# Attention keys written once and copied into both partition halves by DMA, W_u folded during the gates, first biases issued behind V's copies

## The chip, the cores and the metric

The kernel runs on one core of a Trainium2 chip. The metric is the device time of one execution in microseconds (us). The core's engines each run their own list of instructions, in the order of that list: PE (TensorE, matmuls; PEld is its weight loads), DVE (VectorE), ACT (ScalarE), POOL (GpSimd) and SP (SyncE, which here issues DMAs). PSUM tiles (`ps_mm`, `ps_o`, `ps_s`, `ps_t`) hold matmul results.

## The reference

One layer of an encoder over two request groups that share the weights, a prompt of 1024 tokens and a sample of 512, each with 16 meta tokens in front; width 1024, all in float32. Cut to what matters:

```python
h = rmsnorm(x, g_mix)
z = h @ w_in                        # 1024 -> 3*512 + 512 + 2*1024
q, k, v, u, gate_na, gate_fn = split(z)
# 8 heads of 64. A grid token (64 columns a row) attends to the nearest
# 8 rows x 16 columns and the 16 meta tokens; scores have a bias by offset.
y_na = neighbourhood_attention(q, k, v, rel_bias, meta_bias) @ w_branch_na
# u in 4 groups of 128 channels: real part of the 2-D DFT over positions and channels
y_fn = fourier_mix(u) @ w_branch_fn
mixed = sigmoid(gate_na) * y_na + sigmoid(gate_fn) * y_fn
x = x + mixed @ w_out
a = relu(rmsnorm(x, g_mlp) @ w_up)
y = rmsnorm(x + (a * a) @ w_down, g_final)[16:]     # meta tokens dropped
```

## The kernel before

Every float32 factor is kept as two tiles, a rounded high part and the rest (`hi` and `lo`, or `kh` and `kl`), and a product is three matmuls: hi x hi, hi x lo, lo x hi (`mm3`, L120; within attention L491 to L493). Splitting a result out of PSUM takes one instruction on ACT for hi (L131) and one on DVE for lo (L132).

The sample's layer runs first, then the prompt's. Its stages: norm and transpose; V's projection; attention; the gates; `merge_na`, which multiplies attention's output by its branch weights; the Fourier branch (`fourier_channels`, `fourier_positions`); `merge_fn`; the output projection and the MLP.

**Attention** goes over four pairs of heads, `pr` 0 to 3. The generator `project(pr)` makes queries and keys of a pair: the key product in chunks (two of 264 columns for the sample, three of 352, 344 and 344 for the prompt), then the query product, 512 columns at a time. Each head's keys are needed in both halves of the 128 partitions, since a query tile packs two rows of blocks there. A pair has eight units per row block (two heads by four column blocks `j`). A unit is: two matmuls for the scores (L588, L589); on DVE the bias is added (L593), ACT takes the exponential (L595), DVE the reciprocal and the scaling (L596, L597); PE transposes the result (L601), ACT and DVE copy it from PSUM (L131, L132), and PE multiplies by V (L618). These steps of different units are interleaved by `step` with fixed lags, and between them `feed` advances a second chain of work, the next pair's `project` or, in the last pair, extra work: `fold_u` and some column blocks of the gates done early (`early_gates`, as many as `quota` says).

V is written to DRAM (`vd_sample`), spread there into block order (`spread_v`, L692, `vf_sample`), and read back per unit (L555, `vr`). The bias tile `bm` of a unit is a DMA from a prepared table (L706).

**The folds** multiply weights by other weights. `fold_u` multiplies W_u by the channels' DFT matrix: 2 MB of W_u in tile `wuT`, eight groups of four matmuls (L244), each split by three instructions on ACT and three on DVE, two stores of 256 KB a group to the DRAM tiles `wu`. It works in a pool of its own (`fold`) that is open during sample attention. `folded` reads `wu` back through DMAs that POOL issues (L787). `fold_fn` (L756) adds and subtracts two weight tables on DVE: eight blocks `dm`, each with two loads of 256 KB (`in_w_fnA`, `in_w_fnB`), two DVE instructions (L765) and a store to `wfn` (L767). It is one of the generators of the list `beside`, each of which the gates advance once per block `dm`.

**What sets the order.** A tile scheduler takes the program and puts each engine's instructions into a fixed order when the kernel is built; pools' lifetimes and buffer counts bear on it. SP issues nearly all DMAs, one after the other; POOL issues some. `self.behind(marks)` keeps what is written in its block behind the marked instructions.

The key part of `project` writes every chunk, per head, into both halves by engine instructions, for each half `hp`:

```python
nc.scalar.copy(out=flat[hh][hp, gs], in_=src[:, m:])
nc.vector.tensor_tensor(out=flat[2 + hh][hp, gs], in0=src[:, m:],
                        in1=flat[hh][own, gs].bitcast(F32), op=ALU.subtract)
```

and for the first chunk two more for the meta tokens' copies (L527, L532).

Of the kernel before, what the change touches and what calls it, by code (L numbers as in the profile page):

```python
# [17 lines left out]
F32 = mybir.dt.float32  # L18
# [4 lines left out]
ALU = mybir.AluOpType  # L23
# [45 lines left out]
class Layer:  # L69
# [163 lines left out]
    def fold_u(self, p):  # L233
# [3 lines left out]
        dm = p.tile([128, 128], F32, name="dftc")  # L237
        nc.sync.dma_start(dm, self.ins["dft_ch"])
        wuT = p.tile([128, 4, D], F32, name="wuT")
        nc.sync.dma_start(wuT, self.ins["w_uT"].rearrange("(g p) d -> p g d", p=128))  # L240
        for kt in range(8):
            ps = self.psum("mm")
            for g in range(4):
                nc.tensor.matmul(ps[:, g * 128:(g + 1) * 128], wuT[:, g, kt * 128:(kt + 1) * 128], dm,  # L244
                                 start=True, stop=True)
            psv = ps.rearrange("p (g c) -> p g c", g=4)
            hi = p.tile([128, 512], F32R, name="wu_hi", bufs=2)
            lo = p.tile([128, 512], F32R, name="wu_lo", bufs=2)
# [79 lines left out]
    def run(self, order):  # L328
# [3 lines left out]
        for i, (name, T) in enumerate(order):  # L332
# [20 lines left out]
            else:  # L353
                w0 = self.qk_weights(0, [[att.tile(s, F32R, name=n, tag=n, bufs=4).rearrange(
                    "p a b -> p (a b)" if n == "kh" else "p a -> p a")[:, :D].rearrange("p (a b) -> p a b", a=8)
                    for _ in range(2)] for n, s in (("kh", [128, T // 64 + 2, 64]), ("q", [128, T]))])
# [117 lines left out]
    def attention(self, p, name, T, hT, w0, after):  # L474
# [22 lines left out]
        def project(pr):  # L497
# [3 lines left out]
            kh = [p.tile([128, nslot, 64], F32R, name="kh", tag="kh", bufs=4) for _ in range(2)]  # L501
            kl = [p.tile([128, nslot, 64], F32R, name="kl", bufs=4) for _ in range(2)]
            state[pr] = (qs, kh, kl)
            for t in kh + kl:
                for s in (0, nslot - 1):
                    nc.gpsimd.tensor_copy(t[:, s, 16:64].rearrange("p (g c) -> p g c", g=2)[:, :, 0:8],
                                          self.zero[:, None, 0:8].to_broadcast([128, 2, 8]))

            def copies(t, q):

                return bass.AP(t.tensor, t[q].offset, [list(t[q].ap[0]), [(nslot - 1) * 64, 2], [24, 3], [1, 16]])

            for ci, (c0, cn) in enumerate(kch):
                ps = self.psum("mm" if pr else None)
                yield from product(ps[:, :cn], wk, slice(c0, c0 + cn))
                m = NM if ci == 0 else 0
                t0 = 64 + c0 + m - NM
                gs = slice(t0, t0 + cn - m)
                flat = [t.rearrange("p s c -> p (s c)") for t in kh + kl]
                for hh in range(2):  # L520
                    own = slice(64 * hh, 64 * hh + 64)
                    both = own, slice(64 - 64 * hh, 128 - 64 * hh)
                    src = ps[own, :cn]
                    for hp in both:
                        nc.scalar.copy(out=flat[hh][hp, gs], in_=src[:, m:])
                        if m:
                            nc.scalar.copy(out=copies(kh[hh], hp), in_=src[:, None, None, :m].to_broadcast([64, 2, 3, 16]))  # L527
                    for hp in both:
                        nc.vector.tensor_tensor(out=flat[2 + hh][hp, gs], in0=src[:, m:], in1=flat[hh][own, gs].bitcast(F32),
                                                op=ALU.subtract)  # L530
                        if m:
                            nc.vector.tensor_tensor(out=copies(kl[hh], hp), in0=src[:, None, None, :m].to_broadcast([64, 2, 3, 16]),  # L532
                                                    in1=copies(kh[hh], own).bitcast(F32), op=ALU.subtract)
                yield
# [35 lines left out]
        def unit(pr, hh, R, j, blk, shared):  # L570
# [10 lines left out]
            qs, kh, kl = state[pr]  # L581
            bm = p.tile([128, wide], F32, name="bm", bufs=8 if T == 512 else 4)
            self.bias(bm, h, j, w, b)
# [4 lines left out]
            nc.tensor.matmul(ps[:, :W], qs[hh][:, qc], kh[hh][:, kw[0], kw[1]], start=True, stop=False)  # L588
            nc.tensor.matmul(ps[:, :W], qs[hh][:, qc], kl[hh][:, kw[0], kw[1]], start=False, stop=True)  # L589
# [51 lines left out]
        self.spread_v(name, blocks)  # L641
        for _ in project(0):
            pass
# [3 lines left out]
        quota = (0, 0, 0, 1) if T == 512 else (4, 2, 2, 4)  # L647
# [13 lines left out]
        for pr in range(4):  # L661
            nxt = chain(project(pr + 1) if pr < 3 else after, islice(early, 8 * quota[pr]))
            steps = 8 * (quota[pr] + (T // 512 + len(kch) if pr < 3 else 1)) + 4
# [820 lines left out]
```

## Time and profile before

| | |
|---|---|
| runs | 2087.53, 2093.07, 2096.18 us; median 2093.07 |
| profiled execution | 2095.71 us; span 2093.9 us, mean granted clock 0.985 |
| PE busy | 2012.8 us, 96% of the span |
| DVE, ACT, POOL busy | 1115.2, 717.0, 801.3 us |
| sample attention, pairs 0 to 3 | begin 70.0, 95.0, 119.0, 143.2 us; end 180.3 us |
| sample gates, then merge_na | 180.3 to 270.6 us, to 293.0 us |
| prompt attention | about 820 to 1040 us |
| DMA queues, share of 16 engines | hardware (SP) 246.24 MB, 37.8%; software (POOL) 15.37 MB, 3.0% |

How to read it: a row of the timeline has the start, the duration, the engine, the line, the operation, its tile written from its source tiles, the shape, the number of instructions and, in brackets, how long the engine was idle ahead of it and for what. Matmuls overlap in a pipeline, so the price of one is the distance between starts, not its duration. A table by stage gives busy time of each engine in each stretch, the granted TensorE clock (1.00 is full), and the share of time that the DMA engines were busy. A row of DMA queues or issues gives the time from issue to landing. Idle time of an engine matters only where PE waits for it.

### The profile page before, as it was taken

What the parts mean: (1) busy time and instruction counts of PE and PEld (TensorE: products, weight loads), DVE (VectorE), ACT (ScalarE), POOL (GpSimd) and SP (SyncE); (2) the same over time, 40 slices, a digit from 0 to 9 for tenths busy, and PEclk for the clock granted to TensorE, in tenths of its full rate; (3) what the DMA queues carried; (4) which work ended last, traced back from release to release, by engine and by line L of the source; (5) the groups of instructions that cost most, each with busy time, mean ns of one, the idle gap of its engine ahead of it and who ended that gap; (6) DMA issues with size and microseconds to landing.
All of it is one profiled execution on the core that took longest, in us unless ns stands there. A gap on an engine that the chain in (4) does not pass through costs nothing.

```text
span 2093.9 us, 26781 instructions
## 1 busy us (share of the span) xinstructions
PE 2012.8 (96%) x9803; PEld 1670.9 (80%) x9803; DVE 1115.2 (53%) x2073; ACT 717.0 (34%) x1311; POOL 801.3 (38%) x690
## 2 busy tenths in 40 slices
PE   6888999999999999999999999999999999999997
PEld 4777787878888878888878897877888888888886
DVE  6576035556565454577661328374333336556567
ACT  3563323333332223566542213143333332112112
POOL 3233635243443421333433226026777662222220
PEclk9989999999999999999999999999999999999999
DMA  6647753233433344434453452332333225323322
GB/s 205 195 125 219 210 157 112 71 118 106 127 92 91 101 151 173 114 108 116 130 185 116 130 153 91 131 101 86 107 109 121 94 97 203 109 91 101 101 87 95
DMA packets 244755, 263.32 MB, mean 126 GB/s; under 512 B 40904, under 2 KB 195272, under 8 KB 244456
## 3 DMA queue, kind: packets, MB, share of 16 engines
q1 hardware_dynamic: 231856, 246.24, 37.8%
q0 software_dynamic: 12768, 15.37, 3.0%
q8 instruction: 77, 1.26, 0.3%
q14 instruction: 54, 0.44, 0.1%
HBM read 212.08 MB, written 57.56 MB: 129 GB/s over the span
## 4 chain that ended last, share of the span: by engine, by line
PE 83%; DMA 5%; DVE 5%; issue 2%; ACT 2%; POOL 2%; SPq 0%; DVEq 0%; POOLq 0%; ACTq 0%
PE ps_mm L127 24%; PE ps_o L127 23%; PE ps_s L127 20%; PE ps_t L127 4%; PE ps_mm L491 3%; PE ps_mm L492 2%; PE ps_mm L493 2%; PE ps_o L618 2%; DMA raw<-in_w_fnB 1%; PE ps_t L601 1%; POOL w_lo L151 1%; DMA wfn<-raw 1%; DMA w_raw<-in_w_out 1%; PE ps_t L192 1%; PE ps_s L588 0%
## 5 line engine op out<-in xcount | busy, mean ns | idle before, releaser
L151 POOL TENSOR_TENSOR w_lo<-w_raw,w_hi 128x1024 fp32r<-128x1024 f32 x141 | 349.8, 2485 | 661.2 <-ACT w_hi L150 625.2
L150 ACT CAST w_hi<-w_raw 128x1024 fp32r<-128x1024 f32 x142 | 147.3, 1048 | 276.8 <-DMA w_raw<-in_w_up 78.6
L1026 DVE TENSOR_TENSOR relu<-relu 128x512 f32<-128x512 f32 (+1 forms) x34 | 78.9, 2322 | 120.6 <-ACT relu L1025 120.6
L491 PE MATMUL ps_mm<-hT,w_hi 128*128 128x512 f32 (+3 forms) x304 | 118.4, 390 | 0.6 <-DVE wu_lo L132 0.6
L150 ACT CAST h_hi<-w_raw 128x1024 fp32r<-128x1024 f32 x30 | 31.5, 1049 | 230.9 <-DMA w_raw<-hidden_prompt 77.2
L493 PE MATMUL ps_mm<-hT,w_lo 128*128 128x512 f32 (+3 forms) x304 | 109.9, 361 | 0.0
L492 PE MATMUL ps_mm<-hT,w_hi 128*128 128x512 f32 (+3 forms) x304 | 109.8, 361 | 0.0
L1391 DVE TENSOR_TENSOR acc<-acc,ps_mm 128x512 f32<-128x512 f32 x86 | 59.0, 686 | 38.7 <-PE ps_mm L127 38.7
L595 ACT ACTIVATE sc<-sc,ast 128x288 f32<-128x288 f32 (+4 forms) x96 | 53.9, 561 | 74.8 <-DVE ast L593 74.6
L1391 DVE TENSOR_TENSOR acc<-acc,ps_s 128x512 f32<-128x512 f32 x85 | 58.3, 686 | 39.5 <-PE ps_s L127 39.5
L1391 DVE TENSOR_TENSOR acc<-acc,ps_o 128x512 f32<-128x512 f32 x85 | 58.3, 686 | 39.4 <-PE ps_o L127 39.3
L1232 POOL TENSOR_TENSOR x<-w_hi,x 128x512 fp32r<-128x512 f32 (+1 forms) x42 | 63.8, 1518 | 39.6 <-ACT x L1235 39.6
L618 PE MATMUL ps_o<-pt,vb 104*64 104x128 f32 (+6 forms) x576 | 70.2, 255 | 6.5 <-DVE pt L132 4.8
L618 PEld LDWEIGHTS ps_o<-pt,vb 104*64 104x64 f32 (+6 forms) x576 | 65.1, 170 | 13.7 <-DVE pt L132 7.1
L559 POOL TENSOR_TENSOR vb<-vr,vb 96x384 fp32r<-96x384 f32 (+4 forms) x48 | 47.9, 1011 | 54.1 <-ACT vb L558 53.6
L593 DVE CUSTOM_DVE_ANT_0 sc<-ps_s,bm 128x288 f32<-128x288 f32 (+4 forms) x96 | 46.4, 483 | 36.4 <-PE ps_s L589 23.4
L127 PE MATMUL ps_t<-gate,x 128*128 128x512 f32 x264 | 65.3, 396 | 0.0
L493 PEld LDWEIGHTS ps_mm<-hT,w_lo 128*128 128x128 f32 x304 | 58.4, 192 | 7.8
L127 PE MATMUL ps_mm<-gate,x 128*128 128x512 f32 x256 | 64.2, 395 | 0.0
L127 PE MATMUL ps_s<-w_hi,h_hi 128*128 128x512 f32 x160 | 62.2, 389 | 0.0
L127 PE MATMUL ps_s<-w_lo,h_hi 128*128 128x512 f32 x160 | 62.2, 389 | 0.0
L127 PE MATMUL ps_o<-w_hi,h_hi 128*128 128x512 f32 x160 | 62.2, 389 | 0.0
(636 smaller groups left out, 5530.9 us busy)
## 6 DMA issues: line engine op xcount, KB each, us to landing
w_raw<-in_w_down SPq DMA_DIRECT2D x64, 512.0 KB
w_raw<-in_w_in SPq DMA_DIRECT2D x56, 512.0 KB
w_raw<-in_w_up SPq DMA_DIRECT2D x34, 512.0 KB
w_raw<-hidden_prompt SPq DMA_DIRECT2D x32, 512.0 KB
w_raw<-in_w_out SPq DMA_DIRECT2D x16, 512.0 KB
hidden_prompt<-r_hi SPq DMA_DIRECT2D x16, 512.0 KB
hidden_prompt<-r_lo SPq DMA_DIRECT2D x16, 512.0 KB
w_lo<-in_w_up SPq DMA_DIRECT2D x15, 512.0 KB
```

Source lines behind the costliest of these rows:

```text
L127: self.nc.tensor.matmul(out, a, b, start=(i == 0 and not more), stop=(i == len(terms) - 1), skip_group_check=more)
L150: nc.scalar.copy(out=hi, in_=raw)
L151: (lo_engine or nc.gpsimd).tensor_tensor(out=lo, in0=raw, in1=hi.bitcast(F32), op=ALU.subtract)
L491: nc.tensor.matmul(ps, a[0], b[0], start=(kt == 0), stop=False)
L492: nc.tensor.matmul(ps, a[0], b[1], start=False, stop=False)
L493: nc.tensor.matmul(ps, a[1], b[0], start=False, stop=(kt == 7))
L559: nc.gpsimd.tensor_tensor(out=lo, in0=vs, in1=hi.bitcast(F32), op=ALU.subtract)
L595: nc.scalar.activation(out=sc[:, :W], in_=sc[:, :W], func=AF.Exp, bias=st[:, 0:1], scale=-1.0, accum_out=st[:, 1:2])
L618: nc.tensor.matmul(po[:m, j * 128:(j + 1) * 128], v, x, start=(i == 0), stop=(i == len(ops) - 1))
L1026: nc.vector.tensor_tensor(out=r, in0=r, in1=r, op=ALU.mult)
L1232: self.nc.gpsimd.tensor_tensor(out=to, in0=x, in1=y, op=op)
L1391: nc.vector.tensor_tensor(out=acc[t][:, cs], in0=acc[t][:, cs], in1=ps, op=ALU.add)
```

## The change

- **Keys.** One tile `keys` (128 partitions: two heads by 64; hi and lo; slots; 64 columns; one buffer, in a pool of its own) is written by one ACT and one DVE instruction of 128 partitions per chunk. After the last chunk of a pair POOL issues four DMAs from it to the tiles `k` of the two heads, each into one half of the partitions (64 partitions by 1280 values for the sample, 328 KB; by 2304 for the prompt, 590 KB). The scores read `k`.
- **W_u.** `fold_u` is no longer in attention's chain; it is a generator of `beside`, in tiles that are free there, one group of four matmuls per block of the gates. The pool `fold` is gone. The reload of `wu[1, 1]` stands after the gates instead of before them.
- **Early gates.** `quota` of the sample is 2 in the last pair instead of 1.
- **Biases.** The bias of a unit of the pair's first head is issued behind the end of `spread_v` on SP.

```diff
-    def fold_u(self, p):
+    def fold_u(self, dm, wuT, places):
...
-        dm = p.tile([128, 128], F32, name="dftc")
         nc.sync.dma_start(dm, self.ins["dft_ch"])
-        wuT = p.tile([128, 4, D], F32, name="wuT")
-        nc.sync.dma_start(wuT, self.ins["w_uT"].rearrange("(g p) d -> p g d", p=128))
+        for g in range(4):
+            nc.sync.dma_start(wuT[g], self.ins["w_uT"][g * 128:(g + 1) * 128, :])
...
-            with ExitStack() as fold:
-                after = self.fold_u(fold.enter_context(pool("fold", "right"))) if i == 0 else iter(())
-                od = self.attention(att, name, T, hT, w0, after)
+            with pool(f"keys_{name}", "right") as p:
+                od = self.attention(att, p, name, T, hT, w0)
...
-                wu[1, 1] = self.folded(1, 1, wide())
+                if i == 0:
+                    beside.append(self.fold_u(
+                        mp.tile([128, 512], F32, name="relu", bufs=2)[:, :128],
+                        [t.bitcast(F32) for _ in range(2) for t in flat(self.pair(mp, [128, 2, 512]))],
+                        lambda: flat(self.pair(fn, [128, 4, 128], bufs=4))))
                 beside.append(self.fold_fn(fn))
             near_end = self.gates(T, hT, mixed, sig, lambda pr: self.weights(od[pr], oT[pr]), beside)
...
+                wu[1, 1] = self.folded(1, 1, wide())
...
-                for hh in range(2):
-                    own = slice(64 * hh, 64 * hh + 64)
-                    both = own, slice(64 - 64 * hh, 128 - 64 * hh)
-                    src = ps[own, :cn]
-                    for hp in both:
-                        nc.scalar.copy(out=flat[hh][hp, gs], in_=src[:, m:])
...
+                nc.scalar.copy(out=flat[0][:, gs], in_=ps[:, m:cn])
+                if m:
+                    nc.scalar.copy(out=copies(hi), in_=ps[:, None, None, :m].to_broadcast([128, 2, 3, 16]))
+                nc.vector.tensor_tensor(out=flat[1][:, gs], in0=ps[:, m:cn], in1=flat[0][:, gs].bitcast(F32), op=ALU.subtract)
...
+                if ci == len(kch) - 1:
+                    for hh in range(2):
+                        for half in range(2):
+                            nc.gpsimd.dma_start(ks[hh][64 * half:64 * half + 64], keys[64 * hh:64 * hh + 64])
...
-            self.bias(bm, h, j, w, b)
+            with self.behind(spread if h == 0 else []):
+                self.bias(bm, h, j, w, b)
...
         self.spread_v(name, blocks)
+        spread = self.mark((mybir.EngineType.SP,))
...
-        quota = (0, 0, 0, 1) if T == 512 else (4, 2, 2, 4)
+        quota = (0, 0, 0, 2) if T == 512 else (4, 2, 2, 4)
...
-            nxt = chain(project(pr + 1) if pr < 3 else after, islice(early, 8 * quota[pr]))
+            nxt = chain(project(pr + 1) if pr < 3 else (), islice(early, 8 * quota[pr]))
```

Three places of the built order show what moves. In these rows stand the line, the operation, the tile written and the tiles read, and the shape; lines of the changed kernel have other numbers (scores L586 and L587, the bias's addition L591, fold groups L243, `fold_fn`'s sums L768).

DVE in sample attention, where the next pair's first and second key chunks are split among the units of a pair; before, in pair 0:

```order
L593 ISA ast 128x1
L529 TENSOR_TENSOR kl<-ps_mm,kh 64x248
L532 TENSOR_TENSOR kl<-ps_mm,kh 64x2x3x16
L529 TENSOR_TENSOR kl<-ps_mm,kh 64x248
L532 TENSOR_TENSOR kl<-ps_mm,kh 64x2x3x16
L596 RECIPROCAL ast<-ast 128x1 x2
```

and in the changed kernel, from pair 1:

```order
L522 TENSOR_TENSOR keys<-ps_mm,keys 128x264
L591 ISA sc,ast<-ps_s,bm 128x216
L591 ISA ast 128x1
L594 RECIPROCAL ast<-ast 128x1
L595 TENSOR_SCALAR sc<-sc,ast 128x216
L132 TENSOR_TENSOR pt_1075<-ps_t,pt_1074 96x384
L768 TENSOR_TENSOR raw<-raw 128x256 x2
L591 ISA sc,ast<-ps_s,bm 128x288
```

The key instructions are fewer and twice as wide, and `fold_fn`'s sums, which stood in the gates, have moved up between the units of pairs 0 to 2, its loads and stores on SP with them, though no line of the diff says so.

SP between V's last store and the first read of its copies; before:

```order
L321 DMA vd_sample<-pt_420 128x512
L706 DMA bm<-g_un_273 128x1x256 x2
L706 DMA bm<-g_un_272 128x1x192 x2
L706 DMA bm<-g_un_273 128x1x256 x2
L706 DMA bm<-g_un_272 128x1x192
L321 DMA vd_sample<-pt_448 128x512
L238 DMA dftc<-in_dft_ch 128x128
L240 DMA wuT<-in_w_uT 128x4x1024
L692 DMA vf_sample_24_459<-vd_sample 9x12288 x2
L692 DMA vf_sample_32_462<-vd_sample 9x16384 x2
L144 DMA w_raw<-in_w_in 128x8x128
L555 DMA vr<-vf_sample_24_459 108x4x64
```

and in the changed kernel:

```order
L319 DMA vd_sample<-pt_420 128x512
L298 DMA vd_prompt<-vd_sample 16x2048 x2
L766 DMA raw<-in_w_fnA 128x4x128
L319 DMA vd_sample<-pt_448 128x512
L766 DMA raw<-in_w_fnB 128x4x128
L695 DMA vf_sample_24_459<-vd_sample 9x12288 x2
L695 DMA vf_sample_32_462<-vd_sample 9x16384 x2
L709 DMA bm<-g_un_272 128x1x192
L552 DMA vr<-vf_sample_24_459 108x4x64
L709 DMA bm<-g_un_273 128x1x256
L552 DMA vr<-vf_sample_32_462 96x6x64
L709 DMA bm<-g_un_273 128x1x256
```

The biases and W_u's load have left the place ahead of the spread; W_u's load now stands behind attention's last store. The loads of `fold_fn`'s first block and a small copy for the prompt's V have come in.

PE at the start of pair 3; before:

```order
L588 MATMUL ps_s<-kh,q 128x216
L589 MATMUL ps_s<-kl,q 128x216
L244 MATMUL ps_mm<-dftc,wuT 128x128 x4
L601 MATMUL ps_t<-ident,sc 96x128 x3
L244 MATMUL ps_mm<-dftc,wuT 128x128 x4
L618 MATMUL ps_o<-pt_1568,vb 128x128
```

and, in the changed kernel, the first fold group inside the second block of the gates:

```order
L127 MATMUL ps_s<-hT_81,w_lo 128x512 x2
L243 MATMUL ps_mm<-relu,w_hi 128x128
L127 MATMUL ps_mm<-hT_81,w_hi 128x512
L127 MATMUL ps_mm<-hT_82,w_hi 128x512
L127 MATMUL ps_mm<-hT_81,w_hi 128x512
L127 MATMUL ps_mm<-hT_82,w_hi 128x512
```

The fold's matmuls have left attention, where units of attention stood between them, and stand among the gates' 512-column matmuls.

More of the change, by code (lines that the diff above doesn't have):

```diff
@@ L390, in run @@
                 wide = lambda: self.pair(fn, [128, 4, 260], "wu", 1)
[L391 removed]
+                flat = lambda pair: [t.rearrange("p a b -> p (a b)") for t in pair]
+                if i == 0:
[3 more added lines that the diff above has]
+                        lambda: flat(self.pair(fn, [128, 4, 128], bufs=4))))
                 beside.append(self.fold_fn(fn))
@@ L472, in new_hT, with attention @@
         return [tuple(pool.tile([128, 8, T + extra], F32R, name=f"hT{i}") for i in range(2))]
-    def attention(self, p, name, T, hT, w0, after):
+    def attention(self, p, kp, name, T, hT, w0):
         hT, = hT
@@ L500, in project, with copies @@
             qs = [p.tile([128, T], F32R, name="q", tag="q", bufs=4) for _ in range(2)]
[L501 to L511, printed above, removed]
+            ks = [p.tile([128, 2, nslot, 64], F32R, name="k", tag="k", bufs=4) for _ in range(2)]
+            state[pr] = (qs, ks)
+            hi, lo = (keys[:, i] for i in range(2))
+            flat = [t.rearrange("p s c -> p (s c)") for t in (hi, lo)]
+            def copies(t):
+                return bass.AP(t.tensor, t.offset, [list(t.ap[0]), [(nslot - 1) * 64, 2], [24, 3], [1, 16]])
             for ci, (c0, cn) in enumerate(kch):
@@ L641, in attention @@
         self.spread_v(name, blocks)
+        spread = self.mark((mybir.EngineType.SP,))
+        keys = kp.tile([128, 2, nslot, 64], F32R, name="keys")
+        for s in (0, nslot - 1):
+            nc.gpsimd.tensor_copy(keys[:, :, s, 16:64].rearrange("p i (g c) -> p i g c", g=2)[:, :, :, 0:8],
+                                  self.zero[:, None, None, 0:8].to_broadcast([128, 2, 2, 8]))
         for _ in project(0):
```

29 lines of the change are left out of this document (11 added, 18 removed).

## The prediction

> **What bounds the kernel now.** I read the head of the page first, then the stretches of sample attention, then the waits of PE in them, then PE's own rows.
>
> ```profile
> span 2093.9 us, 26781 instructions
> PE 2012.8 (96%) x9803; PEld 1670.9 (80%) x9803; DVE 1115.2 (53%) x2073; ACT 717.0 (34%) x1311; POOL 801.3 (38%) x690
> ...
> PE   6888999999999999999999999999999999999997
> ...
> PEclk9989999999999999999999999999999999999999
> ```
>
> PE is the bound nearly everywhere: 81.1 us of the span are not PE time. What falls short of a 9 lies in slices 2 to 4 (52 to 209 us) and the first and last. In a table by stage, with V's transfers ahead, pairs 0 to 3 of sample attention, its gates, merge_na, and prompt attention:
>
> ```profile
> core 0: us, PE busy (x) PEld busy (x) DVE busy (x) ACT busy (x) POOL busy (x), PEclk, DMA share, GB/s
> ...
> 56.00:70.00 14.00, 13.97 (x94) 12.70 (x92) 6.35 (x15) 6.18 (x16) 2.41 (x1) 1.00 0.88 324
> 70.00:95.00 25.00, 17.25 (x101) 15.14 (x102) 14.86 (x47) 14.19 (x40) 9.33 (x20) 0.86 0.55 153
> 95.00:119.00 24.00, 21.00 (x154) 19.02 (x154) 19.67 (x60) 17.63 (x49) 9.71 (x21) 0.95 0.47 124
> 119.00:143.20 24.20, 20.88 (x144) 19.25 (x142) 16.25 (x53) 15.75 (x45) 9.21 (x15) 0.90 0.37 93
> 143.20:180.30 37.10, 28.60 (x190) 25.79 (x190) 24.73 (x80) 20.98 (x65) 9.35 (x10) 0.88 0.75 228
> 180.30:270.60 90.30, 87.08 (x362) 69.11 (x362) 27.81 (x59) 30.14 (x46) 52.43 (x31) 0.97 0.73 206
> 270.60:293.00 22.40, 22.40 (x98) 18.00 (x98) 10.95 (x20) 6.38 (x17) 7.00 (x7) 1.00 0.74 216
> 820.00:1040.00 220.00, 214.69 (x1343) 188.49 (x1342) 141.05 (x371) 131.34 (x308) 78.48 (x172) 1.00 0.41 111
> ```
>
> Only the four pairs have slack: 110.3 us with PE busy in 87.7. Prompt attention has PE busy in 97.6%. PE's waits from 70 to 180.3 us, then its rows:
>
> ```profile
> PE ps_t L601 <- DVE sc L597: 9.5, 4, 6.2
> PE ps_s L588 <- DVE q L132: 5.6, 4, 2.6
> PE ps_mm L244 <- DVE wu_lo L132: 5.2, 5, 1.8
> ...
> 69.45 0.28 PE L491 MATMUL ps_mm<-hT,w_hi 128*128 128x264 f32 x1
> 69.57 0.28 PE L492 MATMUL ps_mm<-hT,w_hi 128*128 128x264 f32 x1
> ...
> 80.56 0.87 PE L601 MATMUL ps_t<-ident,sc 128*96 128x128 f32 x3 [6.22 <-DVE sc L597]
> ...
> 82.34 0.42 PE L493 MATMUL ps_mm<-hT,w_lo 128*128 128x264 f32 x1
> ...
> 87.90 0.39 PE L491 MATMUL ps_mm<-hT,w_hi 128*128 128x512 f32 x1
> 88.13 0.39 PE L492 MATMUL ps_mm<-hT,w_hi 128*128 128x512 f32 x1
> ...
> 94.75 0.36 PE L588 MATMUL ps_s<-kh,q 128*128 128x216 f32 x1 [1.06 <-DVE q L132]
> ...
> 158.36 1.13 PE L244 MATMUL ps_mm<-dftc,wuT 128*128 128x128 f32 x8 [0.17 <-DVE wu_lo L132]
> 159.25 0.54 PE L618 MATMUL ps_o<-pt,vb 108*128 108x128 f32 x4
> ...
> 173.45 0.32 PE L588 MATMUL ps_s<-kh,q 128*128 128x216 f32 x1
> ...
> 174.34 0.50 PE L601 MATMUL ps_t<-ident,sc 128*96 128x128 f32 x3
> ```
>
> Starts give the prices at full clock. A key chunk is 24 matmuls 0.12 apart, 2.9 us; a query product, or one early gate, 24 at 0.23, 5.5; a fold group 0.89, so 7.1 for eight; a unit of attention 0.89 (its scores, transposes and output, 173.45 to 174.34), 7.1 a pair. Pairs 1 and 2 each need 2 x 2.9 + 5.5 + 7.1 = 18.4 on PE and take 24.0 and 24.2. Pair 3 needs 7.1 + 7.1 + 5.5 = 19.7 and takes 37.1.
>
> **Part 1: pair 0, V and the biases.** V's spread goes to DRAM and back before the first values exist:
>
> ```profile
> 60.72 9.35 DMA vf_sample<-vd_sample
> 70.12 7.77 DMA vr<-vf_sample
> ```
>
> PE stands still for 6.22 us behind this chain (row 80.56). Now the spread moves 2.0 MB while 2.0 MB of W_u and seven bias loads share the engines (share 0.88 at 324 GB/s, row 56). Both leave this stretch; the first weight loads of fold_fn (0.5 MB) come in. Half the traffic would bring the values some 5 us earlier. Two things hold back: the third bias now stands on SP behind the second load of V's copies, and fold_fn's first sums stand on DVE ahead of the first query splits. Bounds: nothing, if the new queue eats it, and -9.0 (6.2 of stall, and most of the 0.14 x 17.25 = 2.4 of lost clock). I take **-4**, nearer the stall's row, less the late bias.
>
> **Part 2: keys, pairs 1 and 2.** Removed from DVE: a pair's eight subtractions L529 and four L532; from ACT their casts.
>
> ```profile
> L529 DVE TENSOR_TENSOR kl<-ps_mm,kh 64x344 fp32r<-64x344 f32 (+3 forms) x68 | 32.2, 474 | 13.0 <-ACT kh L525 7.1 <-ACT kh L527 4.8
> ...
> L532 DVE TENSOR_TENSOR kl<-ps_mm,kh 64x96 fp32r<-64x96 f32 x28 | 6.9, 247 | 0.0
> ...
> L765 DVE TENSOR_TENSOR raw<-raw x16: 410/419/1279, 175.8 to 237.1; 128x256 f32<-128x256 f32 x16
> ...
> 186.35 0.76 DVE L765 TENSOR_TENSOR raw<-raw 128x256 f32<-128x256 f32 x2 [4.56 <-DMA raw<-in_w_fnB]
> ...
> 230.87 0.76 DVE L765 TENSOR_TENSOR raw<-raw 128x256 f32<-128x256 f32 x2 [9.25 <-DMA raw<-in_w_fnB]
> ...
> 236.74 0.76 DVE L765 TENSOR_TENSOR raw<-raw 128x256 f32<-128x256 f32 x2 [5.11 <-DMA raw<-in_w_fnB]
> ```
>
> That is 8 x 0.42 (264 columns; 0.474 is the mean with longer prompt rows) + 4 x 0.25 = 4.4 us of DVE a pair; two at 0.42 and one at 0.25 replace them, 1.1. So DVE gains 3.3 us a pair of its busy 15 to 20. But since the fold's pool is gone, the order moves fold_fn's sums from the gates up into pairs 0 to 2, 2.3 a pair x 2 x 0.42 = 1.9, and each waits on DVE for a load of fnB, with scores, reciprocals and transposes' copies queued behind it. The load is issued on SP behind the store of the block before, so blocks form a chain: in the gates now, sums two to eight start 186.35 to 236.74, six periods of 8.4 us. In attention the same six periods have 15 units of work beside them, 15 x 3.02 = 45 at the pace now. At 8.4 the chain asks for 50 (5 more than now); its shortest cycle there is one store and load, 230.87 to 236.74 = 5.9, so 35. Bounds: +5 from the chain, and -11.4 if both pairs come down to PE's 18.4. The two nearly cancel; I take **-2**, since the chain at its shorter periods is just faster than the units.
>
> ```profile
> L787 POOL DMA_DIRECT2D w_hi<-wu x4: 740/744/747, 267.3 to 1166.5; - x4
> ...
> DMA to landing us min/median/max: 4.1/5.1/14.3
> ```
>
> The four key copies add a step: issue on POOL (nearest row L787, 0.74 each), then landing, 5.1 in the median. Their cover: the last key matmul of the next pair at 82.34, its first score at 94.75, 12 us of query product and units. Splitting (about 1), two issues (1.5) and 5.1 make 7.6, so they cost **0**. Behind them on POOL stand only bias columns and later copies. Their 1.3 MB a pair ride on a DMA share of 0.37 to 0.55.
>
> [...] No row of this trace shows a 64-partition copy within the chip. [...]
>
> **Part 3: pair 3.** The last rows of attention and the first of the gates:
>
> ```profile
> 177.45 0.40 PE L601 MATMUL ps_t<-ident,sc 128*108 128x128 f32 x2 [2.31 <-DVE sc L597]
> ...
> 180.26 1.16 PE L127 MATMUL ps_o<-hT,w_hi 128*128 128x512 f32 x2
> ```
>
> Out go eight fold groups, 7.1 of PE, with PE's 5.2 of waiting for their splits and 24 splits on each of ACT and DVE; in comes a second early gate of 5.5, whose work fills PE between units. PE needs 7.1 + 2 x 5.5 = 18.1; I give it 20, and the drain after the last score 6 (now 7, of which 2.31 waited). 26 instead of 37.1 is **-11**. Bounds: units at their present 3.0 each plus the drain make 24 + 7 = 31, -6; PE's need with 4 of drain makes 22, -15.
>
> **Part 4: gates.** Eight fold groups in (+7.1), one gate out (-5.5), fold_fn out: +1.6. Their 2 MB of W_u is issued on SP only after attention's last store, the fold starts after one more gate, two products = 11 us later, and 2 MB at that stage's 206 GB/s takes 10. DVE and ACT have 60 us idle of 90 for the splits. Bounds +1.6 (load covered) and +8.5 (load runs 7 us over, shared with other weights); I take **+2.5**. The folded tile wu[1,1] is reloaded on POOL after the gates instead of before them; merge_na's stretch of 22.4 us (row 270.60) lies ahead of its reader and exceeds the longest landing, 14.3: 0.
>
> **Part 5: prompt attention.** Twice the key copies with three chunks' cover, PE at 97.6%: **0**; bounds -3 (the 5.3 of slack there) and +5 (first pair's keys late).
>
> Sum: -4 - 2 - 11 + 2.5 = -14.5. The profiled execution took 2095.71, 2.64 above the runs' median: 2081.2 for its like, **2078.6** against the median 2093.07.
>
> **Rivals.** DVE's wait ahead of fold_fn's sums, in all and in number:
>
> ```profile
>   DMA raw<-in_w_fnB: 29.3, 6
> ```
>
> B, the fold_fn chain holds DVE: pair 0 gives 2 and pairs 1 and 2 lose 5; with -11 and +2.5 that is -5.5, 2087.6. For it speaks that six sums waited 29 us in total for fnB now; against it, that DMA is less loaded in attention (0.37 to 0.55 against 0.73).
>
> C, DVE was what held pairs 1 and 2, and they come down to 18.4: -11.4 in place of -2, 2069.2. Against it speaks the 5.9-us cycle, which alone asks 35 of 15 units where PE would need 35.
>
> D, slower: the keys land late. Scores of both heads wait for copies on POOL; this decides once landing takes over 9.5 us (12 less 1 and 1.5). At the greatest 14.3 it costs 5 in each of pairs 1 to 3, 8 in pair 0 (only a query product and a chunk as cover) and 5 in prompt's first pair: +28, 2106.6. Against it: median 5.1. [...]
>
> That the fold merely moves is a rival too: if the gates give back 8.5, the sum is -8.5, 2084.6; it is held in A and B.
>
> **How the numbers follow.** A (2078.6; own range 2072 to 2085) 0.50, B 0.26, C 0.14, D 0.10. The measurement can tell about 0.5%, 10.5 us, from no change, so faster means under 2082.6: most of A (0.42) and C give 0.56; the rest of A and B, 0.34; D 0.10. The range leaves out D and the far part of B and C: 2066 to 2091.
>
> **What would show it.** Pair 0: the 6.22 wait of ps_t under 3. Pairs 1 and 2: 22 to 24 us each, with DVE's waits for fnB there. Pair 3: about 26, no fold rows. Gates: some 92, and fold matmuls waiting under 2 us for W_u. Scores waiting for `k` from DMA over 2 us in any pair would prove D; pairs of 19 us, C; DVE idle over 10 us behind fnB in attention, B. The forecast is wrong, too, if a load queued behind the moved biases or stores on SP delays V's next copies.

## The result, and the profile after

The changed kernel takes 2140.21 us in the median against 2092.67 for the kernel before (four runs each); the ratio is 1.0232, 95% interval 1.0209 to 1.0255. It is slower by 47.5 us, where 14.5 us of gain were forecast. The profiled execution took 2143.11 us, 47.4 more than that of before, so the two traces show the whole difference. The head of the page after, and its two DMA queues:

```profile
span 2141.2 us, 26629 instructions
...
PE 2026.2 (95%) x9803; PEld 1682.2 (79%) x9803; DVE 1092.0 (51%) x1989; ACT 689.9 (32%) x1228; POOL 809.0 (38%) x662
...
PEclk9877999999999999999999999999999999999999
DMA  6775683233433346755555544223332325332322
...
q1 hardware_dynamic: 232192, 246.77, 37.5%
q0 software_dynamic: 15328, 30.05, 6.3%
```

PE's busy time rose by 13.4 us with the same 9803 matmuls. The granted clock is lower, 0.971 for 0.985 in the mean, most plainly in slices 2 to 4 (53 to 214 us); 6.1 us of the rise lie in pairs 0 to 2 of sample attention, 5.8 in prompt attention and 2.0 in `fourier_channels`. The time in which PE does nothing rose from 81.1 to 115.0. DVE, ACT and the instruction count are lower, as the change says. The software queue (POOL) moves 14.7 MB more, the key copies.

The stages, from the start of the first matmul of one to that of the next, in us of each profiled execution:

| stage | before | after | change | forecast |
|---|---|---|---|---|
| up to the first score | 70.0 | 75.2 | +5.2 | |
| sample pair 0 | 24.7 | 33.3 | +8.6 | -4 with the row above |
| pairs 1 and 2 | 48.5 | 64.7 | +16.2 | -2 |
| pair 3 | 37.0 | 36.1 | -0.9 | -11 |
| gates | 90.2 | 86.8 | -3.4 | +2.5 |
| merge_na | 22.4 | 22.5 | +0.1 | 0 |
| fourier_channels | 23.1 | 27.2 | +4.2 | 0 |
| to the prompt's first score | 508.8 | 514.3 | +5.4 | 0 |
| prompt pair 0 | 64.3 | 71.3 | +6.9 | 0 |
| prompt pairs 1 to 3 | 165.2 | 169.4 | +4.2 | 0 |
| the rest | 1039.6 | 1040.4 | +0.8 | 0 |

Sample attention ends at 209.4 us and not at 180.3. The table by stage of the changed kernel, pairs 0 to 3, the gates, then prompt pair 0 from a second table:

```profile
75.20:108.50 33.30, 19.32 (x99) 17.16 (x99) 10.30 (x37) 10.32 (x29) 11.13 (x22) 0.71 0.81 183
108.50:145.00 36.50, 23.35 (x148) 21.31 (x148) 19.35 (x55) 13.62 (x37) 9.74 (x17) 0.73 0.79 202
145.00:173.30 28.30, 22.55 (x149) 20.77 (x149) 18.32 (x54) 13.64 (x37) 10.03 (x15) 0.86 0.74 183
173.30:209.30 36.00, 27.94 (x149) 23.47 (x150) 19.23 (x54) 17.36 (x43) 12.61 (x13) 0.78 0.44 126
209.30:296.20 86.90, 86.90 (x403) 71.58 (x402) 25.38 (x62) 31.85 (x56) 38.49 (x21) 0.98 0.62 185
...
860.10:931.40 71.30, 67.03 (x375) 58.83 (x376) 31.96 (x85) 31.14 (x71) 23.22 (x45) 0.94 0.61 147
```

DVE is less busy in pair 0 than before, and PE waits more. The DMA share stands at 0.74 to 0.81 in pairs 0 to 2, where it stood at 0.37 to 0.55. Rate times length gives 33.3 x 183 + 36.5 x 202 + 28.3 x 183 = 18.6 MB there, against some 9 MB before (25.0 x 153 + 24.0 x 124 + 24.2 x 93). Of the 9.6 MB more, 5.5 are fold_fn (seven blocks of 768 KB) and 3.9 key copies (three pairs). What PE and then DVE waited for, from 60 to 209 us, and fold_fn's sums on DVE ("issue" stands where the profile shows nothing that ended the wait):

```profile
PE ps_t L599 <- DVE sc L595: 17.7, 3, 10.8
PE ps_s L586 <- DVE q L132: 9.1, 2, 8.3
PE ps_t L599 <- DVE pt L132: 8.4, 5, 3.5
PE ps_s L586 <- DMA k<-keys: 5.0, 1, 5.0
```

```profile
DVE raw L768 <- DMA raw<-in_w_fnB: 17.9, 2, 10.8
DVE ast L594 <- ACT sc L593: 15.8, 16, 6.2
DVE raw L768 <- issue: 13.0, 4, 4.6
DVE sc L591 <- DMA bm<-g_un: 7.7, 2, 6.9
```

```profile
104.83 0.76 DVE L768 TENSOR_TENSOR raw<-raw 128x256 f32<-128x256 f32 x2 [10.83 <-DMA raw<-in_w_fnB]
...
165.33 3.69 DVE L768 TENSOR_TENSOR raw<-raw 128x256 f32<-128x256 f32 x2 [2.34 <-issue]
```

At 104.83 DVE has stood for 10.83 us in front of a sum; PE stands with it, 10.8 us in front of a transpose. The chain after the start; the landing of all key copies; and the page's row of DMA issues for the prompt's (576 KB of 1024 bytes, the 590 KB of above), with their median:

```profile
59.55 5.73 DMA vf_sample<-vd_sample
...
65.71 13.63 DMA bm<-g_un
```

```profile
DMA to landing us min/median/max: 4.9/9.1/17.7
```

```profile
k<-keys POOLq DMA_DIRECT2D x16, 576.0 KB, 9.9
```

V's spread is faster, 5.73 us for 9.35. But the second bias, of 128 KB, now behind it, takes 13.63 us from issue to landing; the first, of 96 KB, is issued at 61.73 us, and DVE, which stands 6.9 us for it, adds it at 78.36. A key copy takes 9.1, not 5.1. The first head's V, which the faster spread was to bring forward, is cast at 78.70 us, 0.8 later than before.

### The profile page after: what moved, and what is told of

Its sections match the earlier page's. It is cut to its first block, busy times and chain, and to the rows that moved or that the text cites. A ratio compares the mean times of both kernels' runs of the same rounds, so it can differ in the third digit from the quotient of the medians.

```text
span 2141.2 us, 26629 instructions
## 1 busy us (share of the span) xinstructions
PE 2026.2 (95%) x9803; PEld 1682.2 (79%) x9803; DVE 1092.0 (51%) x1989; ACT 689.9 (32%) x1228; POOL 809.0 (38%) x662
## 3 DMA queue, kind: packets, MB, share of 16 engines
q1 hardware_dynamic: 232192, 246.77, 37.5%
q0 software_dynamic: 15328, 30.05, 6.3%
## 4 chain that ended last, share of the span: by engine, by line
PE 75%; DMA 8%; DVE 8%; issue 3%; ACT 2%; SPq 1%; POOL 1%; DVEq 0%; ACTq 0%; POOLq 0%
PE ps_mm L127 22%; PE ps_o L127 22%; PE ps_s L127 18%; PE ps_t L127 4%; PE ps_mm L494 2%; PE ps_mm L495 2%; PE ps_mm L496 2%; PE ps_o L616 1%; SPq L709 1%; PE ps_t L599 1%; DMA raw<-in_w_fnB 1%; DMA w_raw<-in_w_in 1%; DMA wfn<-raw 1%; DVE hn L848 1%; DMA bm<-g_un 1%
## 5 line engine op out<-in xcount | busy, mean ns | idle before, releaser
L494 PE MATMUL ps_mm<-hT,w_hi 128*128 128x512 f32 (+3 forms) x312 | 125.7, 403 | 2.1 <-DVE q L132 2.1
L496 PE MATMUL ps_mm<-hT,w_lo 128*128 128x512 f32 (+3 forms) x312 | 115.8, 371 | 0.0
L495 PE MATMUL ps_mm<-hT,w_hi 128*128 128x512 f32 (+3 forms) x312 | 115.5, 370 | 0.0
L599 PE MATMUL ps_t<-ident,sc 128*104 128x128 f32 (+3 forms) x288 | 52.5, 295 | 27.6 <-DVE sc L595 19.2
L591 DVE CUSTOM_DVE_ANT_0 sc<-ps_s,bm 128x288 f32<-128x288 f32 (+4 forms) x96 | 46.2, 482 | 51.3 <-DMA bm<-g 15.0
L494 PEld LDWEIGHTS ps_mm<-hT,w_hi 128*128 128x128 f32 x312 | 63.3, 203 | 4.7 <-issue 2.4
L599 PEld LDWEIGHTS ps_t<-ident,sc 128*104 128x104 f32 (+3 forms) x288 | 36.4, 139 | 38.8 <-issue 20.7
L495 PEld LDWEIGHTS ps_mm<-hT,w_hi 128*128 128x128 f32 x312 | 63.1, 202 | 2.3
```

The lines of the kernel that those rows point to most:

```text
L494: nc.tensor.matmul(ps, a[0], b[0], start=(kt == 0), stop=False)
L495: nc.tensor.matmul(ps, a[0], b[1], start=False, stop=False)
L496: nc.tensor.matmul(ps, a[1], b[0], start=False, stop=(kt == 7))
L599: nc.tensor.transpose(tp[:ck, c * 128:(c + 1) * 128], sc[:, c * ck:(c + 1) * ck], self.ident)
```

## The experiments

Three theories. L: fold_fn's bytes and the key copies together load the DMA engines, and every transfer that attention needs comes late. C: DVE and SP stand in order in fold_fn's chain of load, sum and store; bytes play little part. K: the key copies as such, on 64 partitions, are late and that is the loss. Kernels 1 to 4, 5 to 8 and 9 to 12 each shared the runs of the kernel before; their medians were 2093.4, 2093.2 and 2095.8 us. "Ends at" is the end of sample attention in the profiled execution.

**1. fold_fn held behind attention** (`e1_hold_fn`), the changed kernel with:

```diff
+        self.attended = self.mark()            # at the end of attention
...
             for i in range(2):
-                nc.sync.dma_start(raw[i], self.rows(("w_fnA", "w_fnB")[i], dm * 128))
+                with self.behind(self.attended):
+                    nc.sync.dma_start(raw[i], self.rows(("w_fnA", "w_fnB")[i], dm * 128))
```

> The changed kernel, with fold_fn's loads kept behind the end of attention (as before the change they came there by themselves); key copies, W_u in the gates, early gates and biases as changed. Theory L (load): pairs 0 to 2 of sample attention became limited by DMA, 19 MB instead of 9 MB at about 195 GB/s, and fold_fn's 6 MB are the larger part; without them 13 MB need 67 us, less than the 73 us of before: attention ends near 180 us instead of 209, the prompt keeps its 16 us, the total is about 2108. Theory K (keys): the copies on 64 partitions and scores that wait for them are the loss; attention still ends past 200 us and the total stays over 2130. Theory C (chain): DVE waiting in order for fold_fn's loads is all of the sample's loss, bytes play no part: attention ends near 170 us, total about 2100, and the first wait for the keys stays 5 us.

**2. Keys by ACT and DVE** (`e2_keys_engine`), the changed kernel without its key copies:

```diff
-                nc.scalar.copy(out=flat[0][:, gs], in_=ps[:, m:cn])
...
-                            nc.gpsimd.dma_start(ks[hh][64 * half:64 * half + 64], keys[64 * hh:64 * hh + 64])
...
+                    for hp in both:
+                        nc.scalar.copy(out=fl[0][hp, gs], in_=src[:, m:])
...
```

> The changed kernel with the keys written into both halves by ACT and DVE as before the change, no key copies by DMA; fold_fn stays where the change lets it go (attention). Theory L: 15 MB in pairs 0 to 2, about 77 us; attention ends near 185 to 190 us, the prompt's 16 us are gone, total about 2105. Theory K: all of the loss is gone, total 2093 or below. Theory C: only the first wait and the prompt are gained, attention ends near 200 us, total about 2118.

**3. Key copies alone** (`e3_keys_only`), the kernel before with the `keys` tile and its four copies a pair.

> The kernel before with one part of the change alone: keys written once and copied by four DMAs a pair. W_u's fold, one early gate, biases and fold_fn as before. Theory L: the prompt loses 16 us (it has the same copies as the changed kernel) and the sample 5 to 10 (first keys late, W_u's load beside them): total 2113 to 2118. Theory K: nearly the whole loss, total over 2130. Theory C: prompt alone, about 2109.

**4. Neither** (`e4_hold_engine`), both edits of 1 and 2 in the changed kernel.

> The changed kernel with neither of the two: keys by ACT and DVE as before, fold_fn behind attention; what is left of the change is W_u in the gates, the second early gate and the biases behind V's spread. All theories say faster than before: pair 0 gives 3 to 6, pair 3 about 10, the gates take back 0 to 5: attention ends near 167 us, total 2075 to 2085. Over 2090 would say that W_u's move or the biases cost something too.

| | time, us | ratio to before | pairs 0 to 2 | pair 3 | ends at | gates and merge_na |
|---|---|---|---|---|---|---|
| before | 2092.67 | 1 | 73.2 | 37.0 | 180.3 | 112.6 |
| changed: fold_fn in attention, key copies | 2140.21 | 1.0232 | 98.1 | 36.1 | 209.4 | 109.3 |
| 1: key copies, fold_fn held | 2124.8 | 1.0148 (1.0124 to 1.0173) | 67.1 | 34.1 | 176.1 | 125.4 |
| 2: fold_fn in attention, no key copies | 2102.01 | 1.0037 (1.0020 to 1.0053) | 83.8 | 31.6 | 184.8 | 109.3 |
| 4: neither | 2109.23 | 1.0080 (1.0056 to 1.0103) | 73.5 | 31.1 | 175.9 | 126.7 |
| 3: key copies in the kernel before | 2110.12 | 1.0082 (1.0053 to 1.0111) | 63.6 | 42.6 | 183.9 | 110.1 |

Rows 1, 2, 4 and the changed kernel make a square. Against row 4, key copies alone move the end of attention by 0.3 us, fold_fn alone by 8.9, both by 33.5. The loss in sample attention is thus in the two together, and there the theory K (the copies as such) falls: in run 3 they shorten pairs 0 to 2 by 9.6 us, though the first score comes 7.7 later and pair 3 takes 5.6 more. In the prompt the copies as such do cost: run 1 stands 15.6 us above run 4, and from the end of `fourier_channels` to the end of prompt attention it takes 16.6 us more. Run 3's total, 2110.12, is under what theory L expected (2113 to 2118); the sample lost 3.6 us and not 5 to 10. The table by stage, of run 1 (pairs 0 to 2) and of run 2:

```profile
74.90:99.60 24.70, 18.15 (x99) 16.02 (x99) 11.33 (x36) 10.33 (x30) 10.93 (x22) 0.78 0.81 182
99.60:121.30 21.70, 20.66 (x148) 19.30 (x148) 16.22 (x49) 13.81 (x38) 10.56 (x17) 0.93 0.89 190
121.30:142.00 20.70, 19.60 (x148) 17.91 (x148) 14.97 (x48) 13.79 (x37) 10.05 (x15) 1.00 0.90 192
```

```profile
69.40:98.80 29.40, 17.84 (x99) 15.61 (x99) 14.91 (x47) 13.99 (x39) 8.67 (x16) 0.83 0.63 169
98.80:126.30 27.50, 21.20 (x148) 19.47 (x148) 20.55 (x63) 16.55 (x46) 9.20 (x17) 0.88 0.66 187
126.30:153.20 26.90, 21.42 (x149) 19.53 (x149) 19.49 (x63) 16.42 (x46) 7.92 (x14) 0.88 0.67 181
```

With key copies and no fold_fn the DMA share is already 0.81 to 0.90 and the pairs still run at 20.7 to 24.7 us. By that share there is little room for 5.5 MB more; run 9 below moves more per us at nearly the same share, so the share alone does not prove it. The totals of runs 1 and 4 missed what was expected, 2108 and 2075 to 2085, since none of the theories had the other side of the move: with fold_fn held, the gates, which have W_u's fold now, and merge_na take 125 to 127 us instead of 109. Of run 4's gates and merge_na, PE's waits:

```profile
PE ps_mm L127 <- ACT w_hi L150: 7.4, 1, 7.4
PE ps_mm L127 <- ACT gate L736: 3.7, 1, 3.7
```

Run 4 also shows the moved biases by themselves. The first head's V is cast at 72.41 us, 5.5 earlier than before. With key copies this gain is gone: the cast comes at 78.35 in run 1 and at 78.70 in the changed kernel. And on SP six biases and two weight loads then stand ahead of the second head's V. ACT waits 6.79 us for it, and it is cast 0.7 later than before. Pair 0 takes 28.1 us, 3.3 more than before; how much of that is this wait was not tried by itself:

```profile
72.41 0.40 ACT L560 CAST vb<-vr 108x256 fp32r<-108x256 f32 x1 [0.63 <-DMA vr<-vf_sample]
...
84.28 0.40 ACT L560 CAST vb<-vr 108x256 fp32r<-108x256 f32 x1 [6.79 <-DMA vr<-vf_sample]
```

**5. Bytes without the chain** (`e5_bytes_only`), run 1's kernel with 24 loads of 256 KB that nothing reads, as many bytes as fold_fn's 16 loads and 8 stores:

```diff
+                at = 8 * pr + u
+                if T == 512 and (at == 0 or 9 <= at <= 27 and at % 3 == 0):
+                    with self.behind(self.mark((mybir.EngineType.SP,))):
+                        for s in range(3):
+                            junk = kp.tile([128, 4, 128], F32, name="junk", bufs=6)
+                            nc.sync.dma_start(junk, self.rows(("w_fnA", "w_fnB")[s % 2], max(0, (at - 6) // 3) * 128))
```

> The first experiment (fold_fn behind attention, 2124.8 us) with 24 loads of 256 KB added to SP's queue in sample attention, about where the changed kernel has fold_fn's 16 loads and 8 stores, into six spare tiles that nothing reads: the same 6 MB, but no instruction of DVE that waits for them and no store that waits for DVE. Theory L (bytes load the DMA engines, and all transfers that attention needs come later): attention ends past 195 us, not at 176, total over 2143. Theory C (DVE and SP wait in order for fold_fn's chain; bytes alone do little): attention ends before 185 us, total under 2134.

**6. Half the key bytes** (`e6_half_copies`), the changed kernel with each head's own half written by ACT and DVE:

```diff
-                            nc.gpsimd.dma_start(ks[hh][64 * half:64 * half + 64], keys[64 * hh:64 * hh + 64])
...
+                        nc.gpsimd.dma_start(ks[hh][64 - 64 * hh:128 - 64 * hh], ks[hh][own])
```

> The changed kernel with half the bytes of key copies: ACT and DVE write each head's keys straight into its own half of k, and two DMAs a pair copy them into the other half. Theory L: attention ends about half-way between the run without key copies (184.8) and the changed kernel (209.4), near 195 us, and the prompt loses 7 to 9 instead of 15.5: total 2115 to 2122. Theory K (the latency of a copy, not its bytes, is what scores wait for): nothing changes by more than 5 us, total over 2133.

**7. Biases as before** (`e7_no_bias_behind`), the changed kernel without `with self.behind(spread if h == 0 else [])`.

> The changed kernel without the line that puts the first biases behind V's spread. By the prompt, where pair 0 took 71 us with that line and key copies, 66 with key copies alone and 64 with that line alone, it gives back about 5 there; in sample attention 0 to 8 in pair 0, where seven biases and two weight loads stand on SP ahead of the second head's V: total 2127 to 2136. If the biases were not the cause, 2140.

**9. Deeper buffers** (`e9_deep_raw`), the changed kernel with `bufs=4` for fold_fn's and `fn_weights`' `raw` tiles.

> The changed kernel with four buffers instead of two for fold_fn's tiles, so that a block's loads are issued one block earlier; same bytes, no other change. The bytes alone (fifth experiment) gave 21 of the 33 us that fold_fn costs beside key copies. If the other 12 are DVE waiting in order for fnB (chain), most of them go here: attention ends near 197 to 202 us, total 2128 to 2134. If they are not, attention ends at 207 or later, total 2138 or more.

| | time, us | ratio to before | pairs 0 to 2 | ends at | prompt pair 0 |
|---|---|---|---|---|---|
| changed | 2140.21 | 1.0232 | 98.1 | 209.4 | 71.3 |
| 5: run 1 and idle bytes | 2148.55 | 1.0263 (1.0248 to 1.0278) | 87.6 | 197.6 | 71.3 |
| 6: half copies | 2109.68 | 1.0081 (1.0062 to 1.0100) | 84.9 | 189.3 | 65.8 |
| 7: biases not behind | 2135.65 | 1.0202 (1.0186 to 1.0218) | 95.3 | 203.8 | 66.2 |
| 9: deeper buffers | 2126.93 | 1.0146 (1.0130 to 1.0162) | 86.0 | 195.1 | 69.4 |

Attention ends 33.2 us later in the changed kernel than in run 1. Run 5, with loads that nobody reads, ends 21.5 later than run 1, past the 195 us that theory L asked for; its total is larger than the changed kernel's because fold_fn runs in the gates as well. Run 9 keeps the bytes and lets each load be issued a block earlier: 14.3 us go, somewhat more than expected (an end at 197 to 202 us). Pairs 0 to 2 of run 5, and of run 9:

```profile
75.10:103.90 28.80, 17.30 (x100) 15.53 (x100) 13.59 (x44) 12.78 (x35) 12.03 (x25) 0.74 0.95 201
103.90:131.80 27.90, 23.60 (x149) 22.05 (x149) 12.97 (x40) 11.35 (x32) 9.59 (x15) 0.82 0.69 151
131.80:162.80 31.00, 22.50 (x149) 20.85 (x149) 17.50 (x51) 15.45 (x40) 11.73 (x18) 0.83 1.09 231
```

```profile
74.60:109.90 35.30, 18.52 (x99) 16.16 (x99) 11.30 (x38) 10.24 (x30) 11.19 (x23) 0.69 0.86 202
109.90:139.10 29.20, 23.88 (x149) 21.98 (x149) 21.98 (x59) 13.63 (x38) 10.56 (x17) 0.79 0.89 230
139.10:160.50 21.40, 21.17 (x148) 19.83 (x148) 15.09 (x47) 13.74 (x37) 10.02 (x15) 0.90 0.92 234
```

In run 9 DVE's idle time ahead of the sums falls from 30.9 to 16.8 us, the same engines move 230 to 234 GB/s in pairs 1 and 2, and pair 2 comes to 21.4 us.

Both theories hold a part, but 21.5 and 14.3 are not shares of one sum. Only 15 of run 5's 24 loads are issued within pairs 0 to 2, where the changed kernel issues 22 of fold_fn's 24 loads and stores, and its time goes in other waits than the changed kernel's. Two of them from 70 to 200 us, in run 1 and then in run 5:

```profile
PE ps_s L586 <- DMA k<-keys: 5.2, 1, 5.2
ACT vb L555 <- DMA vr<-vf_sample: 14.9, 3, 8.1
```

```profile
PE ps_s L586 <- DMA k<-keys: 13.5, 3, 6.5
ACT vb L555 <- DMA vr<-vf_sample: 29.2, 5, 10.7
```

The changed kernel has 5.0 and 14.3 us there, no more than run 1. What it has beyond run 1 is DVE's 30.9 us ahead of fold_fn's sums, and its pairs 0 to 2 take 31.0 us more. In runs 2, 6, 9 and the changed kernel that idle time is 11.5, 14.1, 16.8 and 30.9 us, and pairs 0 to 2 take 83.8, 84.9, 86.0 and 98.1. So in the changed kernel the moved bytes cost their time through the chain. The second block's load of fnB from issue to landing, in the chain of the changed kernel, where the four key copies are issued within the same 2 us, and in that of run 2, without copies:

```profile
93.30 11.43 DMA raw<-in_w_fnB
```

```profile
90.46 5.25 DMA raw<-in_w_fnB
```

Not every wait is a late landing: the sum at 142.73 us waited 7.08 us for a load that SP issued only at 139.65. How the loss divides between slow landings and SP's queue was not tried.

Run 6, better than expected (2115 to 2122), takes 20 us from attention and nearly the prompt's whole loss: its pairs 1 and 2 take 111.1 us against 117.1 of the changed kernel and 111.5 before. Run 7 gives back 5.0 us in the prompt's pair 0 and 1.8 in the sample's, as expected. In the prompt's pair 0 of the changed kernel the biases stand behind the spread on SP, which took 13.85 us over issuing the one at 845.86 us; 2.4 MB of keys are issued from 846.3 us on, the DMA share from there to 865.6 us is 0.94, and DVE waited 15.0 us for the next bias.

**10. Reading of attention's output held** (`e10_hold_oT`), the changed kernel with run 1's mark `self.attended` and:

```diff
             if dm in (1, 2, 3, 4):
-                bring(dm - 1)
+                with self.behind(self.attended if T == 512 else []):
+                    bring(dm - 1)
```

> The changed kernel with the reading back of attention's output (o_sample into oT, split on ACT, POOL or DVE) kept behind attention's end. In pair 3 of the changed kernel ACT waited 9.2 us in order for these reads, ahead of exponentials. If that is what ate the forecast -11 of pair 3, it takes 28 to 31 us instead of 36.1, and the gates at most 2 more: total 2132 to 2136. If the units' own latency is what paces pair 3, it stays above 34 and the total at 2140.

ACT's waits from 60 to 209 us in the changed kernel, and pair 3 and the gates of run 10 in the table by stage:

```profile
ACT vb L555 <- DMA vr<-vf_sample: 14.3, 3, 8.0
...
ACT oT_hi L150 <- DMA w_raw<-o_sample: 9.2, 2, 5.6
```

```profile
171.80:196.90 25.10, 23.49 (x149) 20.48 (x150) 17.28 (x54) 15.35 (x41) 7.79 (x10) 0.91 0.36 103
196.90:290.00 93.10, 89.77 (x402) 72.80 (x402) 24.23 (x62) 34.32 (x60) 44.47 (x24) 0.96 0.65 194
```

Pair 3 takes 25.1 us, 11.0 less than in the changed kernel and better than expected (28 to 31); the gates take 6.3 back, where at most 2 were expected. The total is 2136.47 (1.0190, 1.0176 to 1.0204).

**8. Key copies where there is room** (`e8_pairs123_dma`), the kernel before with `by_dma = T == 512 and pr > 0` choosing the copies.

> The kernel before, with key copies by DMA for pairs 1 to 3 of the sample alone; pair 0 and the whole prompt keep their keys by ACT and DVE, and nothing else is changed. With key copies in all pairs, pairs 0 to 2 took 63.6 us instead of 73.2, the first wait for keys cost 7.7, pair 3 took 5.6 longer and the prompt lost 13. Here the first wait and the prompt's loss go. By theory L, which finds room on the DMA engines there (share 0.38 to 0.55 before), 4 to 9 us are gained: total 2084 to 2089, against 2093 before. By theory K (copies late wherever they are) no gain, 2093 or more.

It takes 2090.96 us; the ratio is 0.9985 (0.9974 to 0.9996), barely faster than before and less than expected. Its pairs 0 to 2, pair 3 and gates:

```profile
69.10:93.40 24.30, 16.95 (x99) 14.81 (x99) 10.90 (x37) 10.80 (x31) 10.37 (x16) 0.86 0.72 178
93.40:114.60 21.20, 19.59 (x148) 17.92 (x148) 16.11 (x50) 13.96 (x38) 10.52 (x17) 1.00 0.87 182
114.60:135.00 20.40, 19.38 (x149) 17.91 (x149) 14.68 (x47) 13.60 (x37) 10.46 (x18) 1.00 0.99 203
135.00:177.30 42.30, 28.36 (x189) 25.38 (x190) 25.44 (x80) 21.14 (x65) 10.12 (x10) 0.87 0.72 210
```

Pairs 0 to 2 gain 7.3 us, pair 3 gives back 5.3.

**11 and 12. A better whole, and its control.** `e11_best` adds half copies and run 10's hold to run 8; `e12_before_hold_oT` is the kernel before with that hold alone.

> The kernel before with the parts that the runs speak for: sample pairs 1 to 3 get half copies (own half by ACT and DVE, the other half by one DMA a head), pair 0 and the prompt keep engine writes, and the reading of attention's output is held behind attention. W_u, biases and gates as before. With full copies pairs 0 to 2 took 65.9 instead of 73.2 and pair 3 42.3 instead of 37.0, where ACT waited 5.8 for attention's output. Theory L plus that wait: pairs 0 to 2 about 66 to 68, pair 3 36 to 38, total 2082 to 2088. If pair 3 stays at 42, 2089 to 2092.

> The kernel before with the reading of attention's output held behind attention, nothing else. There ACT waited only 0.5 us for it, so the total should not move by more than 2 us: 2091 to 2095. A gain of more would say that the last run's gain is due to this line and not to the keys.

Both missed: 2104.08 (1.0043, 1.0027 to 1.0059) and 2104.72 (1.0040, 1.0027 to 1.0052). The hold alone shortens attention by 3.7 us and lengthens the gates by 12.1. PE waits there 10.5 us for the casts of their weights on ACT, 3.2 before; these casts now queue with those of the output. Run 12's longest waits of PE in the gates:

```profile
PE ps_mm L127 <- ACT w_hi L150: 5.7, 3, 3.4
PE ps_s L127 <- ACT w_hi L150: 3.3, 1, 3.3
```

Why the same hold costs the gates 6.3 us in run 10 and 12.1 here was not tried. Run 8 is the only version seen that beats the kernel before.

## Why the prediction was wrong

**The step that failed first is the key copies' cost of 0 (part 2), "Their 1.3 MB a pair ride on a DMA share of 0.37 to 0.55".** The share was read for the copies alone. The same part moved fold_fn into these pairs and costed it on DVE only; its bytes were added nowhere. 9 MB and 9.6 MB more, in the 73 us of before, ask for 18.6 / 73.2 = 254 GB/s, where no row of before in attention had over 228 (324 stands only in V's stage, 56 to 70 us). The addition would have put the term in question, and with it the chain's "just faster than the units". Runs 1, 2 and 4 show what stands in their place: in sample attention either load alone costs 0.3 or 8.9 us, both 33.5. With both, DVE stands 30.9 us ahead of fold_fn's sums, 11.5 without the copies. Pairs 1 and 2 took 16.2 us more, where 2 less were forecast.

**The chain's period was taken from the gates.** "At 8.4 the chain asks for 50": its sums two to eight began from 104.8 to 165.3 us, 60.5, after a wait of 10.8 us ahead of the second and with up to 7.1 among the others. The bound of +5 had the mechanism of rival B, and run 9 bears it out, but it was sized at the gates' load. B's 2087.6 was on the right side of the forecast and still 53 us short.

**Landing of 5.1 us** came from row L787, HBM to SBUF at another load; for a copy of 64 partitions it was the author's estimate. It measured 9.1 in the median, 17.7 at most. Rival D put the greatest at 14.3 and was right about the first pairs (waits of 5.0 in the sample, about 4.3 in the prompt) but not about pairs 1 to 3, where no score waited for `k`. Its mechanism, scores that wait for late keys, is 9 of the 47 us. The queues' rows give the copies' price: 30.05 - 15.37 = 14.7 MB in 6.3% x 2141.2 - 3.0% x 2093.9 = 72 us of 16 engines, 204 GB/s; the other queue moves 246.77 MB in 37.5% x 2141.2, 307 GB/s.

**Pair 0, -4:** the mechanism shows only without key copies, where the first head's V came 5.5 us earlier (run 4). In the changed kernel it came 0.8 later: the part on V left out the copies, which are issued at 65 to 67 us beside V's. The rest of the step, what stands on SP behind the biases, was named and not priced: in run 4 ACT waited 6.79 us for the second head's V, and pair 0 took 3.3 more.

**Pair 3, -11:** not got. Run 10 reaches the forecast 26 us (25.1), but only with work moved out that the forecast did not count, and the gates take 6.3 of it back. The scheduler moved the reading of attention's output, work of the gates, into the room on ACT, whose order then waited 9.2 us for DMA. The prediction's step "PE between units" looked at PE's list alone.

**Gates, +2.5:** they came out at -3.4. PE has 403 matmuls there for 362, but was busy 86.9 us for 87.1, so the +7.1 - 5.5 did not show; 3.2 us of waits for the weights' casts are gone. In the changed kernel no matmul waited for W_u's load. What was put at nothing is that fold_fn's departure is worth 16 to 17 us of gates and merge_na once W_u's fold is there (changed against run 1, run 2 against run 4).

**wu[1, 1], 0:** fourier_channels took 4.2 us more; PE waited for it:

```profile
PE ps_mm L127 <- DMA w_lo<-wu: 2.0, 1, 2.0
```

Some 2 us of it are this wait; in the rest PE is busy for longer at a lower clock, 0.94 against 1.00. It was not tried by itself.

**Prompt attention, 0:** it takes 11.1 us more, and the stretch up to its first score 5.4 more: +16.5, a third of the whole loss. In run 2, without key copies, both together are 2.3 us less than before; run 3, key copies alone, has 14.1 of the loss, and run 6, half copies, 2.0. Of it, 4.3 us are PE's wait for `k` and some 5 the biases of run 7; the rest was not taken apart. The prediction had +5 as its bound.

## What to carry to other kernels

When a change moves work between engines, add up the bytes of every stretch as well as its busy time, all the moved pieces together, and compare the rate with the highest that the trace shows there: two loads that each fit can fail together (in sample attention 0.3 and 8.9 us alone, 33.5 with both). Ask the built order what else came into freed room, and look at the in-order queue of each engine it came to, not at PE's alone. Work that was out of the way by accident of a pool's lifetime will move when the pool goes.

## What the runs showed of the hardware

- Copies of 64 partitions within SBUF took the DMA engines 1.5 times as long per byte as the transfers of the other queue (204 and 307 GB/s by packet time), and halving them (run 6) was worth 30 us.
- A load of 256 KB landed 5.25 us after its issue without these copies (run 2) and 11.43 us when it was issued among four of them (the changed kernel).
- In sample pairs 0 and 1, where PE was not busy for 14.0 and 13.2 us in place of 7.8 and 3.0, its granted clock was 0.71 and 0.73 in place of 0.86 and 0.95; over the whole kernel, with as many matmuls, its busy time rose by 13.4 us. In pair 3 the clock was 0.78 in place of 0.88 with 8.1 us of idle time for 8.5, so what set it is not shown.
- A bias of 128 KB took 13.63 us to land in the changed kernel, at a DMA share of 0.80 meanwhile (65.71 to 79.34 us).
